# Fixed byte positions in SBUF for weights, activations and FFN blocks of a float32r decoder trunk

## Chip, core and metric

One core of a Trainium2 chip runs the whole kernel in one launch. The metric is device time in microseconds (us) from launch to end; the kernel before was run three times and the median stands for it. One more execution was taken with the profiler, and all rows below are from that one. The engines are TensorE (PE in the profile, with its weight loads as PEld), VectorE (DVE), ScalarE (ACT), GpSimd (POOL) and SyncE (SP, which only issues DMAs here).

## What is computed

A two-layer decoder trunk over 256 positions of width 1024. Each layer is a half-step SwiGLU, a mixer (layer 0: pooling and differential attention; layer 1: a chunkwise mLSTM) and another half-step SwiGLU, each behind an RMSNorm with a shift, scale and gate that come from a conditioning vector, and a final RMSNorm. Everything is float32.

```python
def modnorm(x, g, shift, scale):
    return rmsnorm(x, g) * (1 + scale[:, None, :]) + shift[:, None, :]

def swiglu(h, w_gate, w_up, w_down):          # 1024 -> 2816 -> 1024
    return (jax.nn.silu(h @ w_gate) * (h @ w_up)) @ w_down

for l in range(DEPTH):                        # DEPTH = 2
    mod = (silu(c) @ w_mod[l] + b_mod[l]).reshape(B, 3, 3, D_MODEL)
    shift, scale, gate = mod[:, :, 0], mod[:, :, 1], mod[:, :, 2]
    h = modnorm(x, norm_g[l, 0], shift[:, 0], scale[:, 0])
    x = x + 0.5 * gate[:, 0, None, :] * swiglu(h, w_ffn_gate[l, 0], w_ffn_up[l, 0], w_ffn_down[l, 0])
    h = modnorm(x, norm_g[l, 1], shift[:, 1], scale[:, 1])
    y = even_mixer(h, ...) if l % 2 == 0 else odd_mixer(h, ...)
    x = x + gate[:, 1, None, :] * y
    h = modnorm(x, norm_g[l, 2], shift[:, 2], scale[:, 2])
    x = x + 0.5 * gate[:, 2, None, :] * swiglu(h, w_ffn_gate[l, 1], w_ffn_up[l, 1], w_ffn_down[l, 1])
return rmsnorm(x, final_g)
```

## The kernel before

Activations lie transposed: 128 channels on the partitions, the 256 positions along the free axis. Every large product is cut into units of one 128x128 weight block against one 128x256 block of activations. Weights and activations are both split into a high part (rounded to float32r) and a low part (the rest), and `mm3` (L338) makes three matmuls of a unit: high weight by high activation (L341), low weight by high activation (L342), high weight by low activation (L343). There are 2560 units, so 7680 such matmuls out of 8032 on TensorE. The rest are transposes, statistics and the small products of the mixers.

Weights come in one stream of 160 chunks of 16 units. `split_to` (L285) brings a chunk into a raw tile by DMA from SP, ACT copies it to `wh` (L299), DVE subtracts to get `wl` (L300), two halves ahead of their use. Between them DVE also computes the conditioning columns `modc` from a second stream (`rawm`, L267).

The moving operands of the matmuls are of three kinds:

- `xs`: the normalised input of an FFN or mixer, high and low part, 8 blocks each, 256 columns, written by `norm_x` (L442).
- `xh`, `xl`: the raw input times its scale, not yet divided by the norm, with two extra columns for the shift (258 columns, `XC`). The first 10 blocks of each later projection multiply these while the statistics are still being made, and their results are scaled afterwards (`early`, `evac`). `first_ffn` (L526) uses the same tiles for a normalised input, with 256 columns.
- `hid`: one pool of 46 slots of 258 columns (L153, `slot` L159). `swiglu` (L485) writes the FFN's hidden blocks there, 22 high and 22 low (`hh`, `hl`), which the down projection reads; `split_y` and `gate_h` write the mixers' outputs there; the mixers' temporaries use slots too (`cp` at L891, `gr` at L776, and q, k, v parts by `keep`).

SBUF is filled in the order of the pools: `const` (persistent tiles, in the order in which they are made), `raw` (5 x 8192 bytes per partition), `wh` and `wl` (4 x 4096 each), `hid`, `tmp`, `small`. A tile's size is rounded up to 32 bytes and `const` begins at byte 16512. Adding up the sizes gives each operand's home, its start modulo 512 bytes. The `const` tiles take 62752 bytes, so `wh` begins at byte 120224, which is 416, and since a weight block is 512 bytes per partition all blocks of `wh` and `wl` are at 416. `xs` blocks (1024 bytes apart) are all at 224. `xh[k]` is at 224 + 32k, `xl[k]` at 480 + 32k (1032 bytes rounded to 1056 apart). The 46 `hid` slots are 1056 bytes apart and so lie at all sixteen multiples of 32.

The order of TensorE's instructions is the order in which the units are walked (`sweep`: one output block after another, all k of it in turn), with the mixers' small work dropped between units by lanes (`spawn`, `tick`). In the start phase of `first_ffn` it is turned round: for each k, 16 output blocks run with the same `xh[k]` and `xl[k]`, 48 matmuls with moving operands at one pair of homes.

Of the kernel before, what the change touches and what calls it, by code (L numbers as in the profile page):

```python
# [8 lines left out]
F32 = mybir.dt.float32  # L9
# [5 lines left out]
P = 128  # L15
D = 1024
# [25 lines left out]
NSTART = 8  # L42
NEARLY = 5
START_BLOCKS = [(f, i) for f in range(NSTART) for i in range(2)]

# [91 lines left out]
def trunk_kernel(ctx: ExitStack, tc: tile.TileContext, xT, crow, pack, pack2, wst, mst, outT):  # L137
# [6 lines left out]
    wl_pool = ctx.enter_context(tc.tile_pool(name="wl", bufs=4))  # L144
    hid = ctx.enter_context(tc.tile_pool(name="hid", bufs=46))
    tmp = ctx.enter_context(tc.tile_pool(name="tmp", bufs=2))
    small = ctx.enter_context(tc.tile_pool(name="small", bufs=2))
    ps_one = ctx.enter_context(tc.tile_pool(name="ps_one", bufs=8, space=bass.MemoryType.PSUM))

    uid = [0]  # L150

    def nm(s):
        uid[0] += 1  # L153
        return f"{s}_{uid[0]}"
# [3 lines left out]

    def slot(dt=F32):  # L159
        return hid.tile([P, XC], dt, tag="hid", name=nm("hid"))  # L160

# [3 lines left out]

    pk = const.tile([P, NPACK], F32, name="pk")
    pk2 = const.tile([P, NPACK2], F32, name="pk2")
    cact = const.tile([P, D], F32, name="cact")
    xa = const.tile([P, KT, T], F32, name="xa")
    x = [xa[:, k, :] for k in range(KT)]  # L170
    xh = [const.tile([P, XC], F32R, name=f"xh{k}") for k in range(KT)]
    xl = [const.tile([P, XC], F32R, name=f"xl{k}") for k in range(KT)]
    xs = [[const.tile([P, T], F32R, name=f"xs{k}{i}") for i in range(2)] for k in range(KT)]
    rext = const.tile([P, XC], F32, name="rext")
    ident = const.tile([P, P], F32, name="ident")
    ones = const.tile([P, P], F32, name="ones")
    mhalf = const.tile([P, 2], F32, name="mhalf")
    ghalf = const.tile([P, DEPTH * NSUB * 3 * KT], F32, name="ghalf")
    modc = [const.tile([P, KT], F32, name=f"mod{g}") for g in range(DEPTH * NSUB * 3)]
    masks3 = const.tile([P, 3 * P], F32R, name="masks3")  # L180
    identr = const.tile([P, P], F32R, name="identr")
    maskT = const.tile([P, P], F32, name="maskT")
    tri = const.tile([P, P], F32, name="tri")
    band = const.tile([P, len(WINDOWS), 3 * P], F32, name="band")
    wgh = const.tile([P, 64], F32R, name="wgh")
    wgl = const.tile([P, 64], F32R, name="wgl")

# [186 lines left out]
    def square(k, eng, alone=False):  # L374

        if k == 0:
            stat["acc"], stat["sq"] = tmp.tile([P, T], F32, tag="acc", name=nm("acc")), None
            nc.scalar.activation(stat["acc"], x[k], AF.Square)
            return
        sq = tmp.tile([P, T], F32, tag="sq", name=nm("sq"))  # L380
        nc.scalar.activation(sq, x[k], AF.Square)
        if alone:
            stat["sq"] = sq
        else:
            eng.tensor_tensor(out=stat["acc"], in0=stat["acc"], in1=sq, op=ALU.add)
# [99 lines left out]
    def swiglu(f, hs, gate, bias_g, up, bias_u):  # L485
# [4 lines left out]
        nc.vector.scalar_tensor_tensor(out=h, in0=up, scalar=bias_u, in1=sg, op0=ALU.add, op1=ALU.mult)  # L490
        hh, hl = slot(F32R), slot(F32R)
        nc.scalar.activation(hh[:, 0:T], h, AF.Copy)  # L492
# [33 lines left out]
    def first_ffn(nxt):  # L526
# [50 lines left out]
        for k in range(KT):  # L577
# [6 lines left out]
            a, b = mod_cols(0, 0, k)  # L584
            nc.scalar.activation(xh[k][:, 0:T], xn[k], AF.Identity, bias=b, scale=a)  # L585
            nc.scalar.activation(xn[k], xn[k], AF.Identity, bias=b, scale=a)
            nc.vector.tensor_tensor(out=xl[k][:, 0:T], in0=xn[k], in1=xh[k][:, 0:T].bitcast(F32), op=ALU.subtract)  # L587
            split_to(((k + 1) * nb - 1) // HALF_UNITS)
            for b, _ in order[k * nb:(k + 1) * nb]:
                mm3(out(b), (xh[k][:, 0:T], xl[k][:, 0:T]), k == 0 and b[1] == 0, k == KT - 1, True)  # L590
                if k == KT - 1:
                    done(b)
        look[0] = 2
        with tc.issue_after(last.ins):
            constants()
        gemm(order[KT * nb:], range(KT), lambda k: (xh[k][:, 0:T], xl[k][:, 0:T]), out, done)
        to_x(0, 0, sweep(range(KT), range(NF)), range(NF), lambda f: hs[f], nxt)

    def split_y(src, col):
        yh, yl = slot(F32R), slot(F32R)  # L600
        nc.scalar.activation(yh[:, 0:T], src, AF.Copy, scale=col)  # L601
# [156 lines left out]
    def odd_mixer(l, nxt):  # L758
# [8 lines left out]
        def gates():  # L767
# [7 lines left out]
            nc.vector.tensor_scalar(out=hg, in0=pcol("mlstm_g", 0, 8), scalar1=0.5, scalar2=None, op0=ALU.mult)  # L775
            gr = slot()  # L776
            gb = small.tile([8, 1], F32, tag="gb", name=nm("gb"))
# [97 lines left out]
        def head_v(h):  # L875
# [14 lines left out]
            nc.tensor.matmul(pc[:, 0:NV], lhsT=kTw[h][:, 0:P], rhs=va[:, 0, 0:NV], start=True, stop=True)  # L890
            cp = slot()  # L891
            nc.scalar.activation(cp[:, 0:NV], pc[:, 0:NV], AF.Copy)
# [42 lines left out]
        def gate_h(i, th):  # L935
            while i not in hnT:
# [3 lines left out]
                                           op0=ALU.add, op1=ALU.mult)  # L940
            yh, yl = slot(F32R), slot(F32R)
            nc.scalar.activation(yh[:, 0:T], y, AF.Copy)
# [90 lines left out]
```

## Time and profile before

| | us |
|---|---|
| three runs | 998.0, 998.24, 998.68 (median 998.24) |
| the profiled execution, its own time | 998.09 |
| its span, first to last instruction | 996.4 |
| TensorE busy | 973.5 |
| VectorE busy | 758.1 |
| ScalarE busy | 528.0 |

The span is 1.7 us shorter than the time of the same execution; that rest is launch and end. Matmuls are pipelined and a matmul's recorded duration (about 280 ns) covers several of its neighbours, so a pace, the distance from one matmul's start to the next one's, is read from the first and last start of an unbroken run and the number of matmuls in it, not from durations.

### The profile page before, as it was taken

What the parts mean: (1) busy time and instruction counts of PE and PEld (TensorE: products, weight loads), DVE (VectorE), ACT (ScalarE), POOL (GpSimd) and SP (SyncE); (2) the same over time, 40 slices, a digit from 0 to 9 for tenths busy, and PEclk for the clock granted to TensorE, in tenths of its full rate; (3) what the DMA queues carried; (4) which work ended last, traced back from release to release, by engine and by line L of the source; (5) the groups of instructions that cost most, each with busy time, mean ns of one, the idle gap of its engine ahead of it and who ended that gap; (6) DMA issues with size and microseconds to landing.
All of it is one profiled execution on the core that took longest, in us unless ns stands there. A gap on an engine that the chain in (4) does not pass through costs nothing.

```text
span 996.4 us, 19641 instructions
## 1 busy us (share of the span) xinstructions
PE 973.5 (98%) x8032; PEld 958.8 (96%) x8032; DVE 758.1 (76%) x1201; ACT 528.0 (53%) x872; POOL 217.9 (22%) x223
## 2 busy tenths in 40 slices
PE   7999999999999999999999999999999999999996
PEld 6899999999999999999999999999899999999996
DVE  5979998989879876777798676788867988555452
ACT  3475544448766544444465444445767655444441
POOL 4953220110112322211122222001010113222011
PEclk9999999999999999999999999999999999999998
DMA  9978888875846766766758766676565746565521
GB/s 341 317 295 318 328 329 319 341 284 206 298 155 246 271 245 254 277 252 235 290 182 291 288 245 248 269 293 258 200 223 185 280 171 244 205 229 175 187 105 43
DMA packets 36093, 247.18 MB, mean 248 GB/s; under 512 B 4001, under 2 KB 4385, under 8 KB 7458
## 3 DMA queue, kind: packets, MB, share of 16 engines
q1 hardware_dynamic: 35856, 245.81, 66.7%
q8 instruction: 63, 1.03, 0.4%
q14 instruction: 28, 0.23, 0.1%
q10 hardware_dynamic: 146, 0.11, 0.0%
HBM read 244.86 MB, written 1.05 MB: 247 GB/s over the span
## 4 chain that ended last, share of the span: by engine, by line
PE 82%; DVE 9%; ACT 3%; issue 3%; POOL 1%; DVEq 0%; ACTq 0%; POOLq 0%
PE one L343 26%; PE one L341 26%; PE one L342 26%; DVE wl L300 3%; DVE rawm L267 3%; ACT wh L299 1%; DVE xs L447 1%; POOL hr L401 1%; DVE xn L445 1%; PE one L418 0%; DVE xl L587 0%; DVE t L512 0%; DVE h L490 0%; ACT L488 0%; PE one L842 0%
## 5 line engine op out<-in xcount | busy, mean ns | idle before, releaser
L300 DVE TENSOR_TENSOR wl<-raww,wh 128x1024 fp32r<-128x1024 f32 x320 | 395.5, 1239 | 162.4 <-ACT wh L299 161.1
L299 ACT ACTIVATE wh<-raww 128x1024 fp32r<-128x1024 f32 x320 | 337.2, 1056 | 226.7 <-PE one L343 197.3
L341 PE MATMUL one<-xs,wh 128*128 128x256 f32 x976 | 275.3, 282 | 0.0
L342 PE MATMUL one<-xs,wl 128*128 128x256 f32 x976 | 272.9, 280 | 1.0 <-DVE wl L300 1.0
L343 PE MATMUL one<-xs,wh 128*128 128x256 f32 x976 | 273.1, 280 | 0.0
L341 PE MATMUL one<-hid,wh 128*128 128x256 f32 x832 | 233.7, 281 | 0.2 <-ACT hid L601 0.2
L343 PE MATMUL one<-hid,wh 128*128 128x256 f32 x832 | 233.7, 281 | 0.0
L342 PE MATMUL one<-hid,wl 128*128 128x256 f32 x832 | 233.3, 280 | 0.0
L342 PE MATMUL one<-xh,wl 128*128 128x258 f32 (+1 forms) x752 | 207.5, 285 | 3.2 <-DVE wl L300 2.9
L341 PE MATMUL one<-xh,wh 128*128 128x258 f32 (+1 forms) x752 | 208.1, 287 | 1.8 <-ACT xh L585 1.8
L343 PE MATMUL one<-xl,wh 128*128 128x258 f32 (+1 forms) x752 | 204.6, 283 | 0.0
L493 POOL TENSOR_TENSOR hid<-h,hid 128x256 fp32r<-128x256 f32 x88 | 123.3, 1402 | 340.1 <-ACT hid L492 340.1
L342 PEld LDWEIGHTS one<-xs,wl 128*128 128x128 f32 x976 | 183.6, 188 | 1.4 <-DVE wl L300 1.2
L341 PEld LDWEIGHTS one<-xs,wh 128*128 128x128 f32 x976 | 183.0, 187 | 1.2 <-issue 1.0
L343 PEld LDWEIGHTS one<-xs,wh 128*128 128x128 f32 x976 | 183.1, 188 | 0.0
L341 PEld LDWEIGHTS one<-hid,wh 128*128 128x128 f32 x832 | 156.8, 188 | 0.4 <-ACT hid L601 0.4
L343 PEld LDWEIGHTS one<-hid,wh 128*128 128x128 f32 x832 | 156.6, 188 | 0.2 <-DVE hid L602 0.2
L342 PEld LDWEIGHTS one<-hid,wl 128*128 128x128 f32 x832 | 156.7, 188 | 0.0
L267 DVE CUSTOM_DVE_ANT_0 rawm<-rawm,cact,pk 128x1024 f32<-128x1024 f32 x112 | 150.5, 1371 | 0.0
L342 PEld LDWEIGHTS one<-xh,wl 128*128 128x128 f32 x752 | 140.6, 191 | 5.4 <-DVE wl L300 5.2
L341 PEld LDWEIGHTS one<-xh,wh 128*128 128x128 f32 x752 | 140.3, 191 | 4.1 <-ACT xh L585 2.3
L343 PEld LDWEIGHTS one<-xl,wh 128*128 128x128 f32 x752 | 138.8, 189 | 0.2 <-DVE xl L587 0.2
(222 smaller groups left out, 727.0 us busy)
## 6 DMA issues: line engine op xcount, KB each, us to landing
raww<-wst SPq DMA_DIRECT2D x152, 1024.0 KB, 4.8
rawm<-mst SPq DMA_DIRECT2D x71, 1024.0 KB, 4.9
raww<-wst SPq DMA_DIRECT2D x16, 512.0 KB, 6.4
xa<-xT SPq DMA_DIRECT2D x2, 512.0 KB, 4.7
rawm<-mst SPq DMA_DIRECT2D x2, 512.0 KB, 7.4
outT<-fin SPq DMA_DIRECT2D x3, 256.0 KB, 2.8
pk<-pack SPq DMA_DIRECT2D x1, 416.0 KB, 6.9
outT<-fin SPq DMA_DIRECT2D x2, 128.0 KB, 2.3
```

The lines of the kernel that those rows point to most:

```text
L267: nc.vector.tensor_tensor_reduce(out=ri, in0=ri, in1=cact, scale=factor, scalar=first, op0=ALU.mult, op1=ALU.add, accum_out=modc[n // KT][ ...
L299: nc.scalar.activation(whs[i], src, AF.Copy)
L300: ins = nc.vector.tensor_tensor(out=wls[i], in0=src, in1=whs[i].bitcast(F32), op=ALU.subtract)
L341: nc.tensor.matmul(out, lhsT=wh, rhs=rh, start=start, stop=False, skip_group_check=skip)
L342: nc.tensor.matmul(out, lhsT=wl, rhs=rh, start=False, stop=False, skip_group_check=skip)
L343: nc.tensor.matmul(out, lhsT=wh, rhs=rl, start=False, stop=stop, skip_group_check=skip)
L401: nc.gpsimd.tensor_tensor(out=r, in0=v, in1=mhalf[:, 0:width], op=ALU.pow)
L445: nc.vector.scalar_tensor_tensor(out=xn, in0=x[k], scalar=a, in1=r, op0=ALU.mult, op1=ALU.mult)
L447: nc.vector.scalar_tensor_tensor(out=to[1], in0=xn, scalar=b, in1=to[0].bitcast(F32), op0=ALU.add, op1=ALU.subtract)
L493: nc.gpsimd.tensor_tensor(out=hl[:, 0:T], in0=h, in1=hh[:, 0:T].bitcast(F32), op=ALU.subtract)
```

## The change

Only positions in SBUF change, and what shares a pool. The tiles of `const` are made in another order, with fill tiles between them, so that `xh` and `xl` blocks start at 128 or 160 modulo 256, all high parts `xs[k][0]` at 448 modulo 512, all low parts `xs[k][1]` at 192, and the pools behind (`raw`, `wh`, `wl`) at 0. The `hid` pool becomes two pools of 23 slots of 1024 bytes, one at 448 and one at 192, with `skip` tiles of 192 and 256 bytes ahead of them; pairs of high and low part take one slot of each (`slots()`), single tiles take them by turns. A slot is now 256 columns wide, so the two tiles that need 257 or 258 (`gr`, `cp`) move to the `acc` tag of `tmp`, which is widened. `first_ffn` writes its normalised input to `xs` instead of `xh` and `xl`. Adding up the sizes as above gives the stated homes: `xh[k]` and `xl[k]` both at 128, 160, 384, 416, 128, 160, 384, 416 for k = 0 to 7. No instruction is added to or taken from any engine, and no order is changed.

```diff
+CONST_BASE = 16512
+RAW_PHASE, HIGH_PHASE, LOW_PHASE = 128, 448, 192
+SKIP = 192
...
-    hid = ctx.enter_context(tc.tile_pool(name="hid", bufs=46))
     tmp = ctx.enter_context(tc.tile_pool(name="tmp", bufs=2))
     small = ctx.enter_context(tc.tile_pool(name="small", bufs=2))
+    skip = ctx.enter_context(tc.tile_pool(name="skip", bufs=1))
+    hids = [ctx.enter_context(tc.tile_pool(name="hid0", bufs=23))]
+    skip2 = ctx.enter_context(tc.tile_pool(name="skip2", bufs=1))
+    hids.append(ctx.enter_context(tc.tile_pool(name="hid1", bufs=23)))
...
-    def slot(dt=F32):
-        return hid.tile([P, XC], dt, tag="hid", name=nm("hid"))
+    turn = [0]
+
+    def slot(dt=F32, i=None):
+
+        if i is None:
+            i = turn[0] = 1 - turn[0]
+        return hids[i].tile([P, T], dt, tag="hid", name=nm("hid"))
+
+    def slots():
+        return slot(F32R, 0), slot(F32R, 1)
...
+    modc, xh, xl = [], [], []
+    for i in range(2 * KT):
+        if i % 2 == 0:
+            up_to(RAW_PHASE, 256)
+        (xh if i < KT else xl).append(fixed(f"x{i}", XC, F32R))
+        if i % 2 == 1 and len(modc) < DEPTH * NSUB * 3:
+            modc += [fixed(f"mod{len(modc) + j}", KT) for j in range(6)]
+    mhalf = fixed("mhalf", 2)
+    wgh = fixed("wgh", 64, F32R)
+    up_to(HIGH_PHASE, 512)
+    xs = [[fixed(f"xs{k}", T, F32R)] for k in range(KT)]
+    wgl = fixed("wgl", 64, F32R)
+    up_to(LOW_PHASE, 512)
+    for k in range(KT):
+        xs[k].append(fixed(f"xs{k}l", T, F32R))
+    pk = fixed("pk", NPACK)
...
+    up_to(0, 512)
+    fill(skip, SKIP, "skip")
+    fill(skip2, (LOW_PHASE - HIGH_PHASE) % 512, "skip2")
...
-            stat["acc"], stat["sq"] = tmp.tile([P, T], F32, tag="acc", name=nm("acc")), None
+            stat["acc"], stat["sq"] = tmp.tile([P, XC], F32, tag="acc", name=nm("acc"))[:, 0:T], None
...
-        hh, hl = slot(F32R), slot(F32R)
+        hh, hl = slots()
...
-            nc.scalar.activation(xh[k][:, 0:T], xn[k], AF.Identity, bias=b, scale=a)
+            nc.scalar.activation(xs[k][0], xn[k], AF.Identity, bias=b, scale=a)
             nc.scalar.activation(xn[k], xn[k], AF.Identity, bias=b, scale=a)
-            nc.vector.tensor_tensor(out=xl[k][:, 0:T], in0=xn[k], in1=xh[k][:, 0:T].bitcast(F32), op=ALU.subtract)
+            nc.vector.tensor_tensor(out=xs[k][1], in0=xn[k], in1=xs[k][0].bitcast(F32), op=ALU.subtract)
...
-            gr = slot()
+            gr = tmp.tile([P, XC], F32, tag="acc", name=nm("gr"))
...
-            cp = slot()
+            cp = tmp.tile([P, XC], F32, tag="acc", name=nm("cp"))
```

`fixed(name, w)` makes a `const` tile and counts its rounded size; `up_to(phase, mod)` fills until the count is at `phase` modulo `mod`; `fill` makes a tile that nothing reads.

## Rows read from the trace of the kernel before

**Rows 1.** The page: span, busy time by engine, granted clock in 40 slices.
```profile
span 996.4 us, 19641 instructions
...
PE 973.5 (98%) x8032; PEld 958.8 (96%) x8032; DVE 758.1 (76%) x1201; ACT 528.0 (53%) x872; POOL 217.9 (22%) x223
...
PEclk9999999999999999999999999999999999999998
```

**Rows 2.** The page: the chain that ended last, shares of the span by engine.
```profile
PE 82%; DVE 9%; ACT 3%; issue 3%; POOL 1%; DVEq 0%; ACTq 0%; POOLq 0%
```

**Rows 3.** Groups of TensorE's instructions by shape: count | busy us, mean ns | idle before.
```profile
L341 PE MATMUL one<-xs,wh 128*128 128x256 f32 x976 | 275.3, 282 | 0.0
...
L341 PE MATMUL one<-hid,wh 128*128 128x256 f32 x832 | 233.7, 281 | 0.2 <-ACT hid L601 0.2
L341 PE MATMUL one<-xh,wh 128*128 128x258 f32 x400 | 115.1, 288 | 0.0
...
L341 PE MATMUL one<-xh,wh 128*128 128x256 f32 x352 | 93.0, 285 | 1.8 <-ACT xh L585 1.8
```

**Rows 4.** Line 343 in unbroken stretches: count, min/median/max ns, first and last start.
```profile
L343 PE MATMUL one<-xs,wh x271: 279/279/282, 332.9 to 428.3; 128*128 128x256 f32 x136
L343 PE MATMUL one<-hid,wh x175: 277/280/287, 150.6 to 212.1; 128*128 128x256 f32 x175
L343 PE MATMUL one<-hid,wh x175: 276/281/287, 429.0 to 490.7; 128*128 128x256 f32 x175
L343 PE MATMUL one<-hid,wh x58: 277/281/288, 280.9 to 301.2; 128*128 128x256 f32 x58
L343 PE MATMUL one<-xl,wh x215: 277/279/283, 73.9 to 149.9; 128*128 128x256 f32 x108
L343 PE MATMUL one<-xl,wh x57: 278/283/289, 310.8 to 331.0; 128*128 128x258 f32 x57
L343 PE MATMUL one<-xl,wh x14: 280/282/288, 212.8 to 217.5; 128*128 128x258 f32 x14
```

**Rows 5.** Timeline, start phase: 1st and 30th of 30 matmuls, k = 3, 4, 6, 7.
```profile
41.57 0.28 PE L343 MATMUL one<-xl,wh 128*128 128x256 f32 x1
...
45.01 0.28 PE L343 MATMUL one<-xl,wh 128*128 128x256 f32 x1
...
47.73 0.28 PE L343 MATMUL one<-xl,wh 128*128 128x256 f32 x1
...
51.15 0.28 PE L343 MATMUL one<-xl,wh 128*128 128x256 f32 x1
...
60.13 0.28 PE L343 MATMUL one<-xl,wh 128*128 128x256 f32 x1
...
63.61 0.28 PE L343 MATMUL one<-xl,wh 128*128 128x256 f32 x1
...
66.06 0.28 PE L343 MATMUL one<-xl,wh 128*128 128x256 f32 x1
...
69.48 0.28 PE L343 MATMUL one<-xl,wh 128*128 128x256 f32 x1
```

**Rows 6.** Timeline, odd mixer: first and last of 17 consecutive matmuls on xs.
```profile
719.32 0.28 PE L342 MATMUL one<-xs,wl 128*128 128x256 f32 x1
...
721.13 0.28 PE L343 MATMUL one<-xs,wh 128*128 128x256 f32 x1
```

**Rows 7.** Timeline, gates of the odd mixer, 8-column weights: first matmul of k = 0 to 3.
```profile
688.53 0.28 PE L772 MATMUL one<-xh,wgh 128*8 128x258 f32 x1
...
688.88 0.28 PE L772 MATMUL one<-xh,wgh 128*8 128x258 f32 x1
...
689.24 0.28 PE L772 MATMUL one<-xh,wgh 128*8 128x258 f32 x1
...
689.59 0.28 PE L772 MATMUL one<-xh,wgh 128*8 128x258 f32 x1
```

**Rows 8.** Lines 892 and 897: first and last start of cp's writes and reads.
```profile
L892 ACT ACTIVATE hid<-one x4: 380/386/388, 729.0 to 755.7; 128x257 f32<-128x257 f32 x4
...
L897 PE MATMUL one<-hid,hid x8: 378/378/379, 733.9 to 757.4; 128*128 128x257 f32 x8
```

**Rows 9.** Stretch of the first down projection: busy us (count) by engine, clock, DMA.
```profile
150.00:212.00 62.00, 62.00 (x529) 62.00 (x528) 54.43 (x80) 29.22 (x38) 6.17 (x7) 1.00 0.84 320
```

More of the change, by code (lines that the diff above doesn't have):

```diff
@@ L164, in scol @@
         return small.tile([P, w], F32, tag=n, name=nm(n), **kw)
[L166 to L169, printed above, removed]
-    x = [xa[:, k, :] for k in range(KT)]
-    xh = [const.tile([P, XC], F32R, name=f"xh{k}") for k in range(KT)]
-    xl = [const.tile([P, XC], F32R, name=f"xl{k}") for k in range(KT)]
-    xs = [[const.tile([P, T], F32R, name=f"xs{k}{i}") for i in range(2)] for k in range(KT)]
@@ L174, in trunk_kernel @@
[L174 to L186, printed above, removed]
+    at = [CONST_BASE]
+    def fixed(name, w, dt=F32, shape=None):
+        at[0] += -(-w * 4 // 32) * 32
+        return const.tile(shape or [P, w], dt, name=name)
+    def fill(pool, w, name):
+        if w:
+            pool.tile([P, w // 4], F32, name=name)
+    def up_to(phase, mod):
+        w = (phase - at[0]) % mod
+        at[0] += w
+        fill(const, w, nm("fill"))
@@ new lines, in trunk_kernel @@
+    up_to(LOW_PHASE, 512)
+    for k in range(KT):
+        xs[k].append(fixed(f"xs{k}l", T, F32R))
+    pk = fixed("pk", NPACK)
+    pk2 = fixed("pk2", NPACK2)
+    cact = fixed("cact", D)
+    xa = fixed("xa", KT * T, shape=[P, KT, T])
+    x = [xa[:, k, :] for k in range(KT)]
+    rext = fixed("rext", XC)
+    ident = fixed("ident", P)
+    ones = fixed("ones", P)
+    ghalf = fixed("ghalf", DEPTH * NSUB * 3 * KT)
+    masks3 = fixed("masks3", 3 * P, F32R)
+    identr = fixed("identr", P, F32R)
@@ L188, in pcol @@
+    maskT = fixed("maskT", P)
+    tri = fixed("tri", P)
+    band = fixed("band", len(WINDOWS) * 3 * P, shape=[P, len(WINDOWS), 3 * P])
+    up_to(0, 512)
+    fill(skip, SKIP, "skip")
+    fill(skip2, (LOW_PHASE - HIGH_PHASE) % 512, "skip2")
     def pcol(n, i=0, w=1):
@@ L584, in first_ffn @@
             a, b = mod_cols(0, 0, k)
-            nc.scalar.activation(xh[k][:, 0:T], xn[k], AF.Identity, bias=b, scale=a)
+            nc.scalar.activation(xs[k][0], xn[k], AF.Identity, bias=b, scale=a)
             nc.scalar.activation(xn[k], xn[k], AF.Identity, bias=b, scale=a)
-            nc.vector.tensor_tensor(out=xl[k][:, 0:T], in0=xn[k], in1=xh[k][:, 0:T].bitcast(F32), op=ALU.subtract)
+            nc.vector.tensor_tensor(out=xs[k][1], in0=xn[k], in1=xs[k][0].bitcast(F32), op=ALU.subtract)
             split_to(((k + 1) * nb - 1) // HALF_UNITS)
             for b, _ in order[k * nb:(k + 1) * nb]:
-                mm3(out(b), (xh[k][:, 0:T], xl[k][:, 0:T]), k == 0 and b[1] == 0, k == KT - 1, True)
+                mm3(out(b), xs[k], k == 0 and b[1] == 0, k == KT - 1, True)
                 if k == KT - 1:
@@ L595, in first_ffn @@
             constants()
-        gemm(order[KT * nb:], range(KT), lambda k: (xh[k][:, 0:T], xl[k][:, 0:T]), out, done)
+        gemm(order[KT * nb:], range(KT), lambda k: xs[k], out, done)
         to_x(0, 0, sweep(range(KT), range(NF)), range(NF), lambda f: hs[f], nxt)
     def split_y(src, col):
-        yh, yl = slot(F32R), slot(F32R)
+        yh, yl = slots()
         nc.scalar.activation(yh[:, 0:T], src, AF.Copy, scale=col)
@@ L940, in gate_h @@
                                            op0=ALU.add, op1=ALU.mult)
-            yh, yl = slot(F32R), slot(F32R)
+            yh, yl = slots()
             nc.scalar.activation(yh[:, 0:T], y, AF.Copy)
```

## Prediction, made before the changed kernel was run

> **What bounds the kernel now.** First the page: of a span of 996.4 us TensorE is busy 973.5 us, its clock was granted at nine tenths or more in all slices but the last, and VectorE, the next engine, is busy 758.1 us [rows 1]. Then the chain that ended last: 82% of it are matmuls, and DVE is second with 9% [rows 2]. Then TensorE's groups by shape: three lines of 976 matmuls on `xs`, of 832 on `hid`, of 400 on `xh`/`xl` with 258 columns and of 352 on them with 256, together 7680, with almost no idle time before them [rows 3]. So the kernel's time is 7680 times the pace of one matmul plus some 55 us of start, statistics and small work, and a nanosecond of pace is worth 7.7 us.
>
> The pace is then read stretch by stretch, from line 343, which runs once in three matmuls. On `xs` 271 of them start between 332.9 and 428.3 us: 95.4 us / 270 / 3 = 117.8 ns [rows 4]. 256 columns at 2.4 GHz are 106.7 ns, so each matmul carries 11 ns that its columns don't explain. The duration of these matmuls hardly moves (279 to 282 ns), and VectorE and ScalarE work on and off beside them, so what adds the 11 ns is inside TensorE's own traffic. The other kinds, by the same division: `hid` 61.5/174/3 = 117.8 ns in the first down projection, 61.7/174/3 = 118.2 in the second, 20.3/57/3 = 118.7 behind the even mixer; `xh`/`xl` with 256 columns 76.0/214/3 = 118.4; with 258 columns 20.2/56/3 = 120.2 and 4.7/13/3 = 120.5 [rows 4].
>
> Does the home of an operand set the pace? The start phase is the one place where homes stand still for long: with weights at 416, 30 matmuls of one k. k = 6 (high part at 416) takes 3.48 us for 29 steps, 120.0 ns; k = 3 (320) 3.44, 118.6; k = 4 (352) and k = 7 (448) 3.42, 117.9 [rows 5]. So it does, by some 2 ns from best to worst, and 117.8 is what several homes reach and none of them beats.
>
> **The change, part by part.** What counts is where the new homes stand in that table. If the distance from weight to moving operand decides, the new pair (448 and 192, weights at 0) is the old pair 352 and 96 with weights at 416, which is k = 4. If the moving operand's own place decides, it is 448 and 192, which is k = 7. Both ran at 117.9 by rows of two decimals [rows 5], the same as `xs` runs today. From this:
>
> - *xs*, 2928 matmuls: 117.8 before, 117.8 after. Nothing, ± 0.1 ns or 0.3 us.
> - *hid*, 2496: slots at all sixteen homes become two homes. The first down projection (528) is already at 117.8; the other three (1584) give 0.3 ns each, 0.5 us; the mixers' output projections (384) 0.9 ns, 0.35 us.
> - *x with 256 columns*, 1056: the 672 behind the start phase go from 118.4 to 117.8, 0.4 us. The 384 of the start phase would give about 1 ns each, 0.4 us, but TensorE waits there for the conditioning columns (the idle time before xh is put down to ACT L585) [rows 3], so I take 0 and keep 0.4 for the range.
> - *x with 258 columns*, 1200: the new homes (128 and 384, 160 and 416, both parts alike) have no long run in the trace. One bound: their distances to the weight are 0 and 32 modulo 128, those of k = 6 (120.0) and of k = 3 and 7 (118.6, 117.9) [rows 5]; the mean 119.1 times 258/256 is 120.1, a gain of 0.1 ns and 0.1 us. The other bound: the gates' matmuls, also 258 columns of `xh` and `xl` but with weights of 8 columns, take 0.35 and 0.36 us by turns for three over eight k, 118.3 ns [rows 7], a gain of 1.9 ns and 2.3 us. I take 0.7 us, nearer to the first, whose weights are full blocks.
> - *Two pools for hid*: an FFN holds 22 high and 22 low parts, so one spare slot of each where there were two of any kind; the next pair needs one of each as before. TensorE stood 0.2 us before its 832 high `hid` matmuls in all [rows 3], so nothing now waits for slots, and a down projection's slots come free block by block in its last sweep, before the next FFN writes. Cost 0; if the cover failed, one block's 66 matmuls, 8 us, would be the most that one transition could lose, and I see no mechanism for it.
> - *cp and gr in acc*: two buffers where `cp` had a slot of its own. The third of four `cp` (ACT, 0.39 us each, over 27 us) waits for the first head's last matmul; writes and reads each spread over some 25 us [rows 8], so the one needed is over by two heads' distance. Queued behind that wait on ACT would be the weight halves (L299), so TensorE would be next to wait; nothing of it is due. Cost 0.
> - No instruction, DMA or order changes, and SP's and POOL's queues are as before.
>
> Sum: 0.5 + 0.35 + 0.4 + 0.7 = 1.95 us. The profiled execution took 998.09 us (span 996.4 and 1.7 around it), 0.15 below the median, so 998.1 - 2.0 = **996.1 us**. The bounds of this case: all upper ends (0.4 for the start phase, 2.3 for 258 columns, 0.3 for xs) make 994; all lower ends, 998.
>
> The split weights would still arrive in time: DVE is busy 54.4 of 62 us in the tightest stretch [rows 9], and a pace 0.2% faster asks 0.1 us more of it.
>
> **A rule weighed against the rows.** With weight loads of the same size throughout, the pace was 117.9 at one home and 120.0 at another [rows 5]. The Trainium skill, "TensorE: Matmul & The Clock Gate" (Step-by-step, step 1), says that TensorE reads its stationary and its moving operand through two independent SBUF read ports, so that loading the next weights takes nothing from the running matmul. By that rule the relation of the weights' home to the operands' would be worth nothing, and the sum would be 0 and the time 998.1. The rows differ from the rule at least in that homes do count; that they count through the weights is not shown, since all weights lie at 416.
>
> **The rivals.**
>
> 1. *A better locked state.* In the odd mixer, after the small matmuls of L842, 17 matmuls on the same `xs` and the same weights' homes start between 719.32 and 721.13 us: 1.81/16 = 113 ns [rows 6]. So at unchanged homes TensorE has a second, faster rhythm into which it falls by the moment at which it starts. New homes could make that the usual one. Price: xs 2928 x 4.6, hid 2496 x 5, x256 672 x 5.2 make 13.5 + 12.5 + 3.5, with 0.7 for 258 columns 30 us: 968. For it: the weights' new place, a multiple of 64, isn't in the trace. Against: the long stretches on xs all keep 117.8 [rows 4], and in the start phase no home shows it [rows 5].
> 2. *A worse locked state* (the one on the other side). In the gates the weight home and the x home both move by 32 from one k to the next, so their distance stays, and yet the triples take 0.35, 0.36, 0.35, 0.36 us, the odd k the longer [rows 7]. So the place itself counts, not the distance alone, and the change moves weights and operands from 32 past a multiple of 64 onto one, which is where the odd k stand. With 256 columns the worst constant run is 120.0 against 117.8 [rows 5]: 2.2 x 6480 (xs, hid and x with 256 columns) is 14 us; with the 2.0 us of the sum lost as well, 998.1 + 14 = 1012. It decides from the first matmul with two aligned operands; against it speaks k = 7, whose operands are so aligned and run at 117.9, though with weights at 416.
> 3. *Homes don't matter in the long stretches* (the rule above, or stretches whose pace has other causes than those of the start phase): 998.1, no change. Against it stands the spread between homes [rows 5].
>
> **How the numbers follow.** The forecast's case has 0.52, the better state or a part of it 0.25, the worse 0.15, no effect 0.08. A measurement of this kernel can tell about 0.2%, 2 us, from no change, so the line is at 996.2, and the forecast's case lies half on each side: faster 0.27 + 0.25 = 0.52, same 0.25 + 0.08 = 0.33, slower 0.15. The forecast's own range is 994 to 998. The range over all cases goes from 966 (all of rival 1) to 1000, which leaves out most of rival 2.
>
> **What would show it.** Line 343 on `xs` in a long stretch, divided as above: 117.8 says the forecast, 113 rival 1, 119 to 120 rival 2. `hid` should then have the same pace as `xs` in every down projection, and the minimum and maximum of its durations, 276 and 287 ns now, should close up, as those of `xs` are. The 258-column stretch should read 118.3 to 120.1. The counts on each of lines 341 to 343 should be 1328 on `xs` (976 and the 352 that move there), 832 on `hid` and 400 on `xh` or `xl`. Wrong would be the step from one constant run in the start phase to the long stretches, if `xs` changes its pace though the table says it must not; or new idle time before `hid` matmuls or before ACT L892, which would be the pools.

## The result, and the profile after

The changed kernel took 972.46 us (median of 972.41, 972.28, 972.52 and 973.37), the one before on the same chip 998.21 us: a ratio of 0.9743, with a 95% interval of 0.9726 to 0.976. That is 25.8 us less, where 2.0 were forecast. The profiled execution took 972.41 us, its span is 970.6.

The page first, in the lines that answer to [rows 1, 2]:

```profile
span 970.6 us, 19642 instructions
...
PE 947.3 (98%) x8032; PEld 932.8 (96%) x8032; DVE 757.0 (78%) x1201; ACT 528.2 (54%) x872; POOL 215.9 (22%) x223
...
PEclk9999999999999999999999999999999999999998
...
PE 82%; DVE 9%; ACT 3%; issue 3%; POOL 1%; DVEq 0%; ACTq 0%; POOLq 0%
```

TensorE's busy time fell by 26.2 us with the same 8032 matmuls at the same clock; the chain's shares are what they were, and the other engines' busy times lie within 2 us of theirs. So the same matmuls simply follow one another faster. Which of them, the groups by shape say (`mm3` is now at lines 382 to 384; count | busy us, mean ns | idle before; they answer to [rows 3]):

```profile
L382 PE MATMUL one<-xs,wh 128*128 128x256 f32 x1328 | 364.3, 280 | 1.4 <-ACT xs L626 1.4
...
L382 PE MATMUL one<-hid,wh 128*128 128x256 f32 x832 | 230.2, 277 | 0.4 <-ACT hid L642 0.4
...
L382 PE MATMUL one<-x,wh 128*128 128x258 f32 x400 | 115.8, 290 | 0.0
```

The idle time of TensorE before `hid` is 0.4 us (0.2 before): the two pools cost next to nothing there. Then the paces, from line 382 in unbroken stretches (count, min/median/max ns, first and last start), which answer to [rows 4]:

```profile
L382 PE MATMUL one<-xs,wh x215: 276/276/286, 74.2 to 147.0; 128*128 128x256 f32 x108
L382 PE MATMUL one<-hid,wh x176: 276/276/276, 147.4 to 206.9; 128*128 128x256 f32 x176
L382 PE MATMUL one<-hid,wh x59: 276/276/364, 274.2 to 294.0; 128*128 128x256 f32 x59
L382 PE MATMUL one<-x,wh x58: 278/284/368, 303.4 to 324.2; 128*128 128x258 f32 x58
L382 PE MATMUL one<-xs,wh x271: 276/276/286, 326.0 to 417.8; 128*128 128x256 f32 x136
L382 PE MATMUL one<-hid,wh x176: 276/276/276, 418.1 to 477.6; 128*128 128x256 f32 x176
L382 PE MATMUL one<-hid,wh x64: 281/281/281, 753.1 to 775.4; 128*128 128x256 f32 x64
```

On `xs`, 91.8 us / 270 / 3 = 113.3 ns, where [rows 4] had 117.8. The down projections: 59.5/175/3 = 113.3. Only the odd mixer's output projection, the last row, stayed at 22.3/63/3 = 118.0. With 258 columns it is 20.8/57/3 = 121.6 by this row, which holds one interruption, and 120.7 as the mean over all of them (120.2 before): no gain there. In this kernel the durations are a fingerprint: a stretch of 276/276/276 runs at 113.3 ns, one of 281/281/281 at 117.8. Durations of 279 and 280 don't tell paces apart: 117.8 goes with 279 in [rows 4], and 116.7 with 280 in a run below.

Where the 25.8 us went, by the last start of line 384 (343 before) in each part; "lead" is how far the new kernel is ahead at that point:

| up to the end of | before, us | after, us | lead, us | gained in this part |
|---|---|---|---|---|
| first FFN | 212.4 | 207.1 | 5.3 | 5.3 |
| even mixer's output projection | 301.6 | 294.3 | 7.3 | 2.0 |
| 258 columns | 331.3 | 324.4 | 6.9 | -0.4 |
| up and gate products on `xs` | 428.7 | 418.0 | 10.7 | 3.8 |
| down projection | 491.0 | 477.9 | 13.1 | 2.4 |
| 258 columns | 520.7 | 507.7 | 13.0 | -0.1 |
| `xs` | 616.8 | 600.2 | 16.6 | 3.6 |
| down projection | 679.2 | 660.1 | 19.1 | 2.5 |
| odd mixer | 795.2 | 775.6 | 19.6 | 0.5 |
| 258 columns | 826.5 | 806.9 | 19.6 | 0.0 |
| `xs` | 922.6 | 899.4 | 23.2 | 3.6 |
| down projection | 984.9 | 959.3 | 25.6 | 2.4 |

Some of the rows in [rows 4] end one matmul of line 343 before their stretch does (212.1 there, 212.4 here), which doesn't touch their paces. Every long stretch with 256 columns behind the start phase, the odd mixer's apart, gives 4.4 to 5.0 ns per matmul. Of the 2.0 us up to the even mixer's output projection, 1.1 lie in the mixer ahead of it, where TensorE had stood 0.6 us for ACT (L710 before, behind L705) and now does not.

In the long stretches VectorE keeps up: in the first down projection it is now busy 54.6 of 60 us (columns as in [rows 9], which had 54.4 of 62).

```profile
147.00:207.00 60.00, 60.00 (x532) 60.00 (x531) 54.61 (x80) 29.26 (x38) 5.93 (x7) 1.00 0.87 334
```

In the start phase it doesn't. The last matmuls of k = 6 and 7 start when they did before (63.61 and 69.48 in [rows 5]):

```profile
63.63 0.28 PE L384 MATMUL one<-xs6l,wh 128*128 128x256 f32 x1
...
69.54 0.28 PE L384 MATMUL one<-xs7l,wh 128*128 128x256 f32 x1
```

The matmuls of a row follow one another faster there too (113.4 ns between 47.7 and 52.6 us, where [rows 5] had 117.9 at k = 4), but TensorE spends the gain on waiting for the low weights that VectorE makes. Its waits for them in the first 72 us, before and after (us in total, times, longest):

```profile
PE one L342 <- DVE wl L300: 1.4, 5, 0.4
```

```profile
PE one L383 <- DVE wl L341: 2.9, 8, 0.6
```

So the start phase's 384 matmuls give nothing, and the 5.3 us of the first FFN come from what lies behind them.

One place of the same trace shows both paces on the same operands. In the odd mixer's product on `xs` (timeline: start us, duration us; 20 matmuls, a pair of small ones on each of three lines, then `xs` again):

```profile
734.64 0.28 PE L383 MATMUL one<-xs,wl 128*128 128x256 f32 x1
...
736.79 0.28 PE L384 MATMUL one<-xs6l,wh 128*128 128x256 f32 x1
736.91 0.59 PE L936 MATMUL one<-va,hid 128*128 128x257 f32 x2
...
738.33 0.28 PE L383 MATMUL one<-xs,wl 128*128 128x256 f32 x1
738.45 0.28 PE L384 MATMUL one<-xs7l,wh 128*128 128x256 f32 x1
738.56 0.28 PE L382 MATMUL one<-xs,wh 128*128 128x256 f32 x1
738.68 0.28 PE L383 MATMUL one<-xs,wl 128*128 128x256 f32 x1
738.80 0.28 PE L384 MATMUL one<-xs0l,wh 128*128 128x256 f32 x1
```

2.15/19 = 113.2 ns ahead of the small matmuls, 0.47/4 = 117.5 behind them, and so on to the end of the output projection at 775.4. It is [rows 6] the other way round: there an interruption led into the fast rhythm, here out of it.

Two questions stand: does the operand's own place count or its distance from the weights, and what decides which of two paces a stretch takes?

### The profile page after: what moved, and what is told of

It is laid out like the page before. It is cut to its first block, busy times and chain, and to the rows that moved or that the text cites. A ratio compares the mean times of both kernels' runs of the same rounds, so it can differ in the third digit from the quotient of the medians.

```text
span 970.6 us, 19642 instructions
## 1 busy us (share of the span) xinstructions
PE 947.3 (98%) x8032; PEld 932.8 (96%) x8032; DVE 757.0 (78%) x1201; ACT 528.2 (54%) x872; POOL 215.9 (22%) x223
## 4 chain that ended last, share of the span: by engine, by line
PE 82%; DVE 9%; ACT 3%; issue 3%; POOL 1%; DVEq 0%; ACTq 0%; POOLq 0%
PE one L382 26%; PE one L384 26%; PE one L383 26%; DVE wl L341 3%; DVE rawm L308 3%; ACT wh L340 2%; DVE xn L486 1%; POOL hr L442 1%; PE one L459 0%; DVE t L553 0%; DVE h L531 0%; PE one L705 0%; ACT L529 0%; PE one L703 0%; PE one L883 0%
## 5 line engine op out<-in xcount | busy, mean ns | idle before, releaser
L383 PE MATMUL one<-xs,wl 128*128 128x256 f32 x1328 | 363.3, 278 | 4.1 <-DVE wl L341 4.1
L382 PE MATMUL one<-xs,wh 128*128 128x256 f32 x1328 | 364.3, 280 | 1.4 <-ACT xs L626 1.4
L383 PEld LDWEIGHTS one<-xs,wl 128*128 128x128 f32 x1328 | 248.0, 189 | 6.6 <-DVE wl L341 6.3
L382 PEld LDWEIGHTS one<-xs,wh 128*128 128x128 f32 x1328 | 247.4, 189 | 2.9 <-ACT xs L626 1.7
L382 PE MATMUL one<-x,wh 128*128 128x258 f32 x400 | 115.8, 290 | 0.0
L383 PE MATMUL one<-x,wl 128*128 128x258 f32 x400 | 112.9, 282 | 1.1 <-DVE wl L341 1.1
L384 PE MATMUL one<-x,wh 128*128 128x258 f32 x400 | 113.7, 284 | 0.0
L426 POOL TENSOR_TENSOR acc<-acc,sq 128x256 f32<-128x256 f32 x41 | 34.6, 845 | 259.9 <-ACT sq L422 235.8
L382 PEld LDWEIGHTS one<-x,wh 128*128 128x128 f32 x400 | 76.3, 191 | 1.7 <-issue 1.3
L383 PEld LDWEIGHTS one<-x,wl 128*128 128x128 f32 x400 | 76.4, 191 | 1.3 <-DVE wl L341 1.3
L384 PEld LDWEIGHTS one<-x,wh 128*128 128x128 f32 x400 | 76.0, 190 | 0.3 <-DVE x L433 0.2
L529 ACT ACTIVATE sg<-one 128x256 f32<-128x256 f32 x73 | 27.6, 383 | 73.1 <-PE one L384 73.0
```

The lines of the kernel that those rows point to most:

```text
L382: nc.tensor.matmul(out, lhsT=wh, rhs=rh, start=start, stop=False, skip_group_check=skip)
L383: nc.tensor.matmul(out, lhsT=wl, rhs=rh, start=False, stop=False, skip_group_check=skip)
L384: nc.tensor.matmul(out, lhsT=wh, rhs=rl, start=False, stop=stop, skip_group_check=skip)
L529: nc.scalar.activation(sg, gate, AF.Silu, bias=bias_g)
```

## Experiments: place or distance

In what follows a home is a start modulo 512 bytes, and the distance is the moving operand's home less the weights', modulo 256. Before, `xs` stood at distance 64 and `hid` at all eight; after, both stand at 192. Each kernel up to the table of raw x was run once. The kernel before, run once beside each of the first two sets, took 997.62 us and 994.04 us; its medians elsewhere are 998.21 and 997.93.

**All homes moved by 32.** The distances stay, every place is another, and the weights no longer start at a multiple of 64.

```diff
-RAW_PHASE, HIGH_PHASE, LOW_PHASE = 128, 448, 192
+RAW_PHASE, HIGH_PHASE, LOW_PHASE = 160, 480, 224
-    up_to(0, 512)
+    up_to(32, 512)
```

> The changed kernel with every home moved on by 32 bytes: weights at 32, high parts at 480, low parts at 224, raw x at 160 or 192 modulo 256. All distances between weights and moving operands stay. Theory 'place' (operands that start on a multiple of 64 are what makes the faster rhythm): xs and hid back at 117.8 ns, about 995 us. Theory 'distance' (only moving home minus weight home counts): 113.3 ns as in the changed kernel, 972 us. Theory 'entry' (both rhythms are open to every home, the moment at which a stretch is entered chooses): a mixture of 113.3 and 117.8, between the two times.

Measured: 971.77 us. The same stretch on line 382 (columns as above):

```profile
L382 PE MATMUL one<-xs,wh x271: 276/276/283, 325.9 to 417.7; 128*128 128x256 f32 x136
```

91.8/270/3 = 113.3 again. The place alone is worth nothing.

**The weights alone back at 416.**

```diff
-SKIP = 192
+SKIP = 288
-    up_to(0, 512)
+    up_to(416, 512)
```

> The changed kernel with its weights alone back at 416; x, xs and hid stay at their new homes. Theory 'distance': the distances become those of the start phase's k = 7 before (448 and 192 against 416), which ran at 117.9 ns, so xs and hid at 117.8, about 995 us. Theory 'place', if the weights' place counts: the same 117.8. If the moving operands' place alone counts: 113.3 ns, 972 us.

Measured: 989.27 us, 16.8 more than with the weights at 0, though no moving operand has moved.

```profile
L382 PE MATMUL one<-xs,wh x271: 277/280/280, 330.2 to 424.7; 128*128 128x256 f32 x136
```

94.5/270/3 = 116.7 ns, at distance 32. No theory had this number: it is neither of the two rhythms of distance 192.

**The kernel before with its weights alone at 0**, by 96 bytes of fill ahead of the weight pools (the pools behind them, `hid` too, move along); `xs` stays, and then stands at distance 224.

```diff
+    const.tile([P, 24], F32, name="fill")
```

> The kernel before with its weights alone moved from 416 to 0 (96 bytes of fill ahead of the weight pools); xs stays at 224, hid at all sixteen homes. If the weights' place alone makes the faster rhythm: xs at 113.3 ns, 13 us less, about 985 us, and hid somewhat faster. Theory 'distance': xs stands at 224 from the weights, in place of 320; the start phase's k = 5 before had 480 = 224 modulo 256 and ran at 118.3, so 998 to 1000 us. Theory 'place' for both operands: no gain, 998 us.

Measured: 999.13 us. The same stretch (one line further down, since a line was added):

```profile
L342 PE MATMUL one<-xs,wh x271: 277/280/285, 333.2 to 429.0; 128*128 128x256 f32 x136
```

95.8/270/3 = 118.3, against 117.8 with the weights at 416. The weights' home at 0 is no gain by itself. Both runs that move the weights alone speak against a rule of the Trainium skill, "TensorE: Matmul & The Clock Gate" (Step-by-step, step 1): that stationary and moving operand come through two independent SBUF read ports, so that loading weights takes nothing from the running matmul. Moving only the weights changed the pace of the same matmuls from 113.3 to 116.7 and from 117.8 to 118.3 ns.

**Bare matmuls at every distance.** The whole computation is left out: rows of 48 matmuls (three in the order of `mm3`, high, high and low moving part, here all on one weight block), each row behind a wait for ScalarE, with the weights at 0 or 32 and the moving operands at each multiple of 32. No other engine works beside a row.

> Leaves out the whole computation: only matmuls of one weight block by one moving block, 48 in a row of the pattern high, high, low, for weights at 0 and 32, high operands at each of the sixteen multiples of 32, low operands at the same home or 256 on, 256 columns; and the same with 258 columns and one home. Each row of 48 starts after a wait for ScalarE. No other engine works beside it. Theory 'distance': the pace of weights 0, home m equals that of weights 32, home m + 32, for all m. Theory 'place': with weights at 0 the homes on multiples of 64 are at 113.3, and with weights at 32 none of these is. Theory 'entry': since all rows start alike, the pace is the same pattern for both, and few rows stand at 113.3. For 258 columns all theories expect 118 to 121 ns, none below 118.

The settled pace of a row, 256 columns:

| distance | 0 | 32 | 64 | 96 | 128 | 160 | 192 | 224 |
|---|---|---|---|---|---|---|---|---|
| ns | 120.0 | 117.8 | 117.8 | 120.1 | 118.7 | 117.3 | 117.8 | 118.3 |

With the weights at 32 the same distances give the same paces; whether high and low part stand 256 apart or not made no difference, but for one row at distance 32, which ran at 116.7. With 258 columns the rows lie between 118.7 and 122.2, most between 120.0 and 120.9; there distance 64 gave 118.7 with the weights at 0 and 122.2 with them at 32, so with 258 columns the distance alone doesn't fix the pace. Four rows of the timeline's, second and last low-part matmul of each, 42 matmuls apart (the tile's name says the homes: w weights, m high part, s what the low part adds):

```profile
206.11 0.28 PE L47 MATMUL w0m448s256n256x<-lv,wt 128*128 128x256 f32 x1
...
211.06 0.28 PE L47 MATMUL w0m448s256n256x<-lv,wt 128*128 128x256 f32 x1
...
420.07 0.28 PE L47 MATMUL w32m480s256n256x<-lv,wt 128*128 128x256 f32 x1
...
425.02 0.28 PE L47 MATMUL w32m480s256n256x<-lv,wt 128*128 128x256 f32 x1
...
166.94 0.28 PE L47 MATMUL w0m256s256n256x<-lv,wt 128*128 128x256 f32 x1
...
171.97 0.28 PE L47 MATMUL w0m256s256n256x<-lv,wt 128*128 128x256 f32 x1
...
381.14 0.28 PE L47 MATMUL w32m288s256n256x<-lv,wt 128*128 128x256 f32 x1
...
386.18 0.28 PE L47 MATMUL w32m288s256n256x<-lv,wt 128*128 128x256 f32 x1
```

4.95/42 = 117.9 at distance 192 with the weights at 0 and at 32; 5.03/42 = 119.8 and 5.04/42 = 120.0 at distance 0. So with 256 columns the distance sets the pace, with no help from other engines. But the very distance of the changed kernel gives 117.9 here, and 113.3 there.

## Experiments: one distance, two rhythms

**The changed kernel at distance 64.** Everything as in the change, one home for all, the two pools, but the distance that `xs` had before.

```diff
-RAW_PHASE, HIGH_PHASE, LOW_PHASE = 128, 448, 192
-SKIP = 192
+RAW_PHASE, HIGH_PHASE, LOW_PHASE = 128, 320, 64
+SKIP = 64
```

> The changed kernel with high parts (xs and FFN blocks) at 320 and low parts at 64 in place of 448 and 192, weights at 0 and raw x at 128 or 160 as it has them. 64 modulo 256 is the distance that xs already had in the kernel before (224 against 416), where it ran at 117.8 ns. Theory 'distance alone sets the pace': xs and hid at 117.8, about 995 us. Theory 'two rhythms, the entry chooses' (this distance has both 117.8 and 113.3, as rows 6 showed once, and the stretch of 258 columns ahead of xs, which is as in the changed kernel, decides): 113.3 in the long stretches, 971 to 975 us.

Measured: 995.72 us.

```profile
L382 PE MATMUL one<-xs,wh x271: 278/280/280, 331.4 to 426.8; 128*128 128x256 f32 x136
...
L382 PE MATMUL one<-hid,wh x176: 280/280/280, 427.2 to 489.0; 128*128 128x256 f32 x176
```

95.4/270/3 = 117.8 and 61.8/175/3 = 117.7. The distance alone is 23.3 of the 25.8 us. In the traces, 2.3 us remain against the kernel before up to the last down projection: 1.2 of them in the even mixer ahead of its output projection, where the 0.6 us wait for ACT is gone here too, and 1.1 in the other stretches, from 118.1 to 118.7 ns closing up to 117.8. The kernel before beside this run took 994.04 us, less than the run itself; that run comes up again below.

**Raw x alone at its old distances**: with the weights at 0, the high parts at 320 + 32k and the low parts at 64 + 32k.

```diff
-        if i % 2 == 0:
-            up_to(RAW_PHASE, 256)
+        if i == 0:
+            up_to(320, 512)
...
-        if i % 2 == 1 and len(modc) < DEPTH * NSUB * 3:
-            modc += [fixed(f"mod{len(modc) + j}", KT) for j in range(6)]
+    modc += [fixed(f"mod{j}", KT) for j in range(DEPTH * NSUB * 3)]
```

> The changed kernel with raw x alone at its old distances from the weights (320 + 32k for high, 64 + 32k for low parts); xs and FFN blocks stay at 448 and 192, weights at 0. Theory 'distance alone': xs and hid stay at 113.3; the 258-column stretch goes from 120.7 back to the old 120.2, so 970 to 972 us. Theory 'the entry chooses': the long stretches behind the 258-column blocks may fall back to 117.8, up to 995 us, while the first FFN, which has no such blocks ahead of it, keeps what it has.

Measured: 970.99 us, with the 258 columns at 120.2 ns. So the new homes of raw x are no part of the gain: by this run the old ones do as well. The two short projections changed sides against the changed kernel (the line that reads 382 there is the low weight's here):

```profile
L382 PE MATMUL one<-hid,wl x59: 281/281/281, 274.2 to 294.7; 128*128 128x256 f32 x59
...
L382 PE MATMUL one<-xs,wl x272: 276/276/385, 326.0 to 418.3; 128*128 128x256 f32 x136
...
L382 PE MATMUL one<-hid,wl x64: 276/276/276, 753.0 to 774.4; 128*128 128x256 f32 x64
```

The even mixer's output projection is now at 20.5/58/3 = 117.8, the odd mixer's at 21.4/63/3 = 113.2, though neither reads raw x: what they read stands where it stood. Whether the edit did this is not shown; below, two traces of one kernel differ in the same way.

**Raw x at 64.**

```diff
-RAW_PHASE, HIGH_PHASE, LOW_PHASE = 128, 448, 192
+RAW_PHASE, HIGH_PHASE, LOW_PHASE = 64, 448, 192
```

> The changed kernel with raw x at 64 or 96 modulo 256 in place of 128 or 160. In the bare rows of 258 columns with weights at 0 home 64 ran at 118.7 ns and 96 at 119.9, against 120.0 and 120.1 for 128 and 160. Theory 'constant runs tell the pace': the 258-column stretches 0.7 to 1.5 ns faster, 0.8 to 1.8 us, about 971 us. Theory 'entry': xs may change its rhythm as well, in which case some or all long stretches stand at 117.8 and the time is up to 994 us.

Measured: 975.53 us. The first FFN's stretch and the next one:

```profile
L382 PE MATMUL one<-xs,wh x215: 281/281/281, 74.1 to 149.7; 128*128 128x256 f32 x108
...
L382 PE MATMUL one<-xs,wh x271: 276/276/283, 331.0 to 422.8; 128*128 128x256 f32 x136
```

75.6/214/3 = 117.8 in the first FFN, its down projection too, and 113.3 in the later ones. The first FFN's products read no raw x, so the edited home can't be the direct cause: a whole FFN of 1174 matmuls took the other rhythm, 1174 x 4.4 ns = 5.2 us. The odd mixer, whose output projection ran in the fast rhythm here, gave 1.2 us of it back.

**Bare matmuls behind different beginnings.** The computation is left out again: at each distance rows of 36 matmuls behind a wait alone (z), one float32 matmul (f), 9 matmuls and one of another width (c and its columns), or 9 with 258 columns at another home (r and the home).

> Leaves out the whole computation: bare rows of 36 matmuls of 256 columns (weights at 0, high operand 256 on from the low one) at all eight distances modulo 256, each behind one of several beginnings: a wait alone, a float32 matmul, one float32r matmul of 64 to 384 columns, nine matmuls of 258 columns at one of eight homes. Then rows of 48 of 258 columns that change between two homes. Theory 'distance alone': every distance has one pace whatever stands ahead of it (120.0, 117.8, 117.8, 120.1, 118.7, 117.3, 117.8, 118.3 for 0, 32, ... 224). Theory 'two rhythms, the entry chooses': distances 64 and 192 show 113.3 behind some beginnings and 117.8 behind others, the same beginning giving the same pace in every row. For 258 columns I expect 118.5 to 122 for all pairs.

At distance 192, of 17 beginnings 10 led to 113.3 ns (f, c128, c192, c272, r0, r32, r64, r96, r160, r192) and 7 to 117.8 (z, c64, c240, c320, c384, r128, r224). At distance 64 two of 16 led to 113.3 (c320, r64), the other 14 to 117.8 (f, the first row of the run, isn't counted: it ran at 213 ns until its last eight matmuls). At distance 0 all ran at 120.0. The others: 116.5 to 116.9 (32), 119.9 to 120.2 (96), 118.5 to 118.8 or 120.0 (128), 117.4, 118.6 or 120.0 (160), 118.1 to 118.4 (224). With 258 columns no pair of homes was below 118.7. In the timeline, two low-part matmuls of each row (every third matmul is one):

```profile
120.06 0.28 PE L54 MATMUL d192z0x<-lv,wt 128*128 128x256 f32 x1
...
123.24 0.28 PE L54 MATMUL d192z0x<-lv,wt 128*128 128x256 f32 x1
...
132.16 0.28 PE L54 MATMUL d192c128x<-lv,wt 128*128 128x256 f32 x1
...
135.56 0.28 PE L54 MATMUL d192c128x<-lv,wt 128*128 128x256 f32 x1
...
29.95 0.28 PE L54 MATMUL d64c128x<-lv,wt 128*128 128x256 f32 x1
...
33.48 0.28 PE L54 MATMUL d64c128x<-lv,wt 128*128 128x256 f32 x1
...
79.73 0.28 PE L54 MATMUL d64r64x<-lv,wt 128*128 128x256 f32 x1
...
82.45 0.28 PE L54 MATMUL d64r64x<-lv,wt 128*128 128x256 f32 x1
```

3.18/27 = 117.8 ns (nine low parts of three matmuls) behind a wait, 3.40/30 = 113.3 behind a matmul of 128 columns, on the same operands. At distance 64 the latter beginning gives 3.53/30 = 117.7, and 9 matmuls of 258 columns at home 64 give 2.72/24 = 113.3. So a distance can hold more than one steady rhythm, and the beginning of a row chooses which; at distance 192 the fast one came far more often. Each beginning ran once at a distance, except the wait alone, which ran eight more times at distance 192 in the bare rows above and led to 117.8 each time.

## Experiments: can the rhythm be chosen by raw x?

Four kernels in turn on one chip: the changed one again, and raw x at 0, 32 and 64, each by `RAW_PHASE` alone. The bare rows had shown the 258 columns at their best near distances 0 to 64.

> The changed kernel as it is, for the three that follow and for its spread. If the beginning of a stretch decides its rhythm and the beginnings after a wait vary from run to run, its times should come in steps of what one stretch is worth (646 and 528 matmuls in the first FFN: 5.2 us; 320 in the odd mixer: 1.4 us). If homes alone decide, they agree within about 0.5 us, at 972.

> The changed kernel with raw x at 0 or 32 modulo 256. In the bare rows 258 columns that change between homes 0 and 32 took 119.4 ns, against 121.1 for 128 and 160. If that carries over: 1200 matmuls x 1.3 to 1.7 ns, 1.5 to 2 us below the changed kernel, about 970, provided that the long stretches stay at 113.3. If x's homes act on the rhythm of what follows (258-column beginnings at 0 and 32 both led to 113.3 at distance 192), also the stretch behind the gates may turn fast, 1.4 us more. If bare rows don't carry over: no difference.

> The same with raw x at 32 or 64 modulo 256: 119.4 ns in the bare rows, and beginnings at 32 and 64 both led to 113.3 at distance 192. If that carries over: about 970 us. Otherwise as the changed kernel, 972, or up to 5 us more if the first FFN starts in the slower rhythm.

> Raw x at 64 or 96 again, which took 975.5 us with the first FFN's long stretches (1174 matmuls) at 117.8, though x's homes are not read before these stretches end. If the beginning after a wait differs from run to run, some of its runs are about 5 us faster, 970 to 971. If the homes fix it, all are at 975 to 976.

| raw x at | runs, us | median | ratio to before, 95% | 258 columns, ns |
|---|---|---|---|---|
| 128 (the change) | 972.51, 973.02, 971.36, 971.17 | 971.94 | 0.9739 (0.9723 to 0.9755) | 120.8 |
| 0 | 972.56, 976.11, 976.49, 976.82 | 976.30 | 0.9775 (0.9757 to 0.9794) | 119.5 |
| 32 | 972.31, 975.38, 971.24, 971.25 | 971.78 | 0.9746 (0.9728 to 0.9764) | 119.3 |
| 64 | 976.83, 976.51, 971.97, 976.70 | 976.60 | 0.9776 (0.9754 to 0.9797) | 120.4 |

With raw x at 0, 32 or 64, one kernel takes either of two times, some 4 to 5 us apart. The profiled executions of the second (which took 972.56) and of the fourth (976.83) show the first FFN in different rhythms:

```profile
L382 PE MATMUL one<-xs,wh x215: 276/276/281, 74.4 to 147.1; 128*128 128x256 f32 x108
```

```profile
L382 PE MATMUL one<-xs,wh x215: 281/281/281, 74.0 to 149.6; 128*128 128x256 f32 x108
```

72.7/214/3 = 113.2 ns, and 75.6/214/3 = 117.8.

Two kernels were traced twice without any edit between, and each time one short stretch changed sides. The even mixer's output projection of the changed kernel, 276/276/364 in the first trace, reads in this set's:

```profile
L382 PE MATMUL one<-hid,wh x59: 281/281/365, 274.3 to 294.9; 128*128 128x256 f32 x59
```

That is 20.6 us against 19.8, with one interruption in each. The odd mixer's, with raw x at 64, in the earlier trace and in this set's (taken on another chip):

```profile
L382 PE MATMUL one<-hid,wh x64: 276/276/276, 757.6 to 779.0; 128*128 128x256 f32 x64
```

```profile
L382 PE MATMUL one<-hid,wh x64: 281/281/281, 757.8 to 780.0; 128*128 128x256 f32 x64
```

21.4/63/3 = 113.2 ns, and 22.2/63/3 = 117.5. So the side on which a short stretch falls can change from one run to the next while every home stays.

Raw x at 32 saves 1.5 ns on 1200 matmuls, 1.8 us by that, but the fastest runs of both take 971.2 us. In the traces TensorE waits longer for VectorE's low weights behind the faster 258 columns (between 72 and 820 us 3.0 us at 32, 2.3 at 128), and the trace at 32 gains 0.9 us behind the first FFN; why the fastest runs show nothing of that is open. No version beats the changed kernel by what these runs can tell. Whether the home of raw x shifts the odds of the longer time (one in eight at 128 and 32 together, six in eight at 0 and 64) or whether that is chance stays open; of the seven longer times in the table one was traced.

## Where the prediction was right and where it was wrong

The forecast was 996.1, and the range over all cases held the time only by rival 1, which had a chance of 0.25 with its part results. That the kernel is faster was forecast, but the forecast's own sum is worth a tenth of the gain, and the rest came by a mechanism that it had put at nothing; as far as that sum goes, it is luck that the range held the time. By its steps:

- **xs, "117.8 before, 117.8 after. Nothing".** This is the step that failed, with 113.3 measured. The table of the start phase [rows 5] was right in what it showed, and the distance reading picked the right row: k = 4 is distance 192. What failed was to take one constant run of 30 matmuls as the pace of its home. Distance 192 has two steady paces, 117.8 and 113.3, and k = 4 had fallen into the first. [rows 6] said so much, 113 ns at unchanged homes, and I gave that a quarter because all long stretches on `xs` keep 117.8 [rows 4]; but these stood at distance 64, where the bare rows find the fast rhythm behind 2 of 16 beginnings against 10 of 17 at 192.
- **The sum of the likeliest case, 2.0 us**, is nearly what the kernel at distance 64 gave against before, 998.2 - 995.7 = 2.5 by one run, but half of that lay in the even mixer, which the sum doesn't have. The terms for `hid` and for x with 256 columns were sound for homes that keep the slow rhythm.
- **Rival 1's price, 968**, was right in its mechanism, its gain 4 us too large. The up and gate stretches gave 3.6 us for 814 matmuls each, 4.4 ns and not 4.6; the down projections 4.5 to 4.8 and not 5; the odd mixer stayed slow (0.5 us in all where its 192 output matmuls alone were priced at 1.0); and x with 258 columns, priced at a gain of 0.7, lost half a nanosecond each, 0.6 us.
- **Rival 2**, the parity of the place, falls by the run with all homes moved by 32. The gates by turns [rows 7] must have another cause: with all homes moved by 32 the gates' triples keep their times to 0.01 us, and neither the changed kernel nor that one shows them by turns. What it is stays open; their weight blocks are 8 columns wide.
- **x with 258 columns.** The bounds were 118.3 and 120.1; measured 120.7, outside. No pair of homes in the bare rows shows the gates' 118.3 for full weights.
- **Rival 3**, homes that don't matter in long stretches, falls by the run at distance 64, and the rule of two independent ports by both runs that moved the weights alone.
- **The start phase**, taken at 0, gave 0. But the split weights do not all arrive in time there: its matmuls became faster, and TensorE's waits for VectorE's low weights grew from 1.4 to 2.9 us.
- **The rest beside the 7680 matmuls.** By the prediction's own paces they take 909 us of the span of 996.4, so the rest is some 88 us and not 55. No term of the forecast used it.
- **Costs at zero.** Right: the pools (0.4 us idle before `hid`), and `cp` and `gr` (nothing new in the chain). The counts on each line, 1328, 832 and 400, and the closing up of `hid`'s durations, to 276/276/276, came as said.

That a stretch keeps the rhythm in which it begins, until the next interruption, is shown by the odd mixer in the traces before and after, by the bare rows, and by the first FFN, which ran whole in the one rhythm or the other in two kernels that differ only in raw x. That a kernel's homes don't fix the rhythm is shown by the two kernels that were traced twice. What makes a stall in the one and none in the other, inside TensorE's reads of weights and operands, is not shown by any run here.

One run stands apart: the kernel before once took 994.04 us, beside the second set of experiments. One of its three `xs` stretches of 814 matmuls in the fast rhythm would be 3.6 us; that is argued only, no trace of that run shows it.

## What to carry to other kernels

Where matmuls follow one another without a gap and the pace stands some per cent above what the columns explain, add up the start addresses of weights and moving operand and try their distance modulo 256 bytes: it costs no instruction, and was worth 23 us of 998 here. Take a pace from several stretches with different beginnings before trusting it as the pace of a layout, since a layout can have more than one and a short constant run shows only one of them. And expect such a kernel to move in steps from run to run (here 4 to 5 us, about one FFN): look into the trace which stretch changed its rhythm before blaming or praising an edit.

## What the runs showed of the hardware that was not expected

- Float32r matmuls of 128x128 by 256 columns settle at a few fixed paces: 113.3, 116.7, 117.3, 117.8, 118.3 to 118.7 and 120.0 ns. At 2.4 GHz, 113.3 is 272 cycles, 116.7 is 280 and 120.0 is 288, for 256 columns; nothing ran below 113.3. The Trainium skill, "TensorE: Matmul & The Clock Gate" (Wait — 56ns, not 53.3ns?), gives about 2.5 ns above the columns' time for back-to-back matmuls, as an estimate 109.2 ns here; no stretch with float32r reached that.
- With 256 columns only the difference of the two homes counts, with period 256 bytes (bare rows with the weights at 0 and at 32, one row apart); with 258 columns one distance gave 118.7 and 122.2 ns. The page "SBUF — State Buffer" of the Trainium skill (its list on reading the diagram) says that TensorE never waits on anyone at its SBUF port. The bare rows agree that no other engine is needed for the loss: alone, TensorE ran at 113.3 to 120.0 ns there, where the columns take 106.7 at 2.4 GHz. That its own two reads hold each other up is argued from the distance between them, not shown.
- Two more columns cost more than their time: 258 columns ran at 118.7 ns or more at every home tried, 5.4 ns above the best pace of 256, where two columns are 0.8 ns.
